# A transformer block on one core: x and the per-layer input also handed over with channels on partitions, and one conversion moved at two boundaries

## The chip, the core and the metric

The kernel runs on one core of a Trainium2 chip. The metric is the device time in microseconds of one execution of the whole program, on inputs that lie in the chip's memory. Five engines work side by side, each through its own list of instructions in order: PE (matrix multiply, results into PSUM), DVE (vector), ACT (activations), POOL, and SP, which here only issues transfers. ACT can issue transfers too.

## The reference, cut to what matters

One decoder layer on 256 tokens with 2048 channels, in float32. The part at the front is

    u    = rmsnorm(x, g_mix_pre)          # per token; gain per channel
    proj = u @ w_in[i]                    # 2048 x 10240
    qa, ka, va, qb, kb, vb, ga, gb = split(proj)

Then come two kinds of attention, two branch products that are mixed by sigmoid gates, `w_out`, a residual and a norm, an MLP (`w_up`, squared relu, `w_down`), a residual and a norm, and last `sigmoid(rmsnorm(h) @ w_ple_gate) * (p @ w_ple_proj)` with a norm and a residual, where `p` is the per-layer input, 256 tokens by 256 channels.

## The kernel before

PE contracts over partitions, so an activation has to stand with its channels on partitions. The kernel computes every product with its factors in two parts: a float32 is split into a high part (rounded to the type PE takes at full rate) and a low part (the rest), and three products hi·hi, hi·lo, lo·hi are summed in PSUM.

Weights come in slices of 256 rows by 512 columns (512 KB), `raw`, into a pool of five buffers (`NRAW`). `head` makes the high part `whi` on ACT, `low` the low part `wlo` on DVE; these have eight buffers. A *chunk* is one product of 512 output columns; with 2048 channels it has eight *steps* s = 0..7, each of one raw slice, and each step has two halves m = 0, 1 (128 tokens each). A half is six matmuls, so a step is twelve. `run` walks the steps; ahead of each half it calls the chunk's `hook(s, m)`, then `ensure`, which issues loads and conversions in order up to a slice ahead of the step, then the matmuls, then the functions of the chunk's `script`. Nothing reorders: the order in which Python calls the engines is the order on each engine, and semaphores do the rest. Transfers take eight semaphores in turn, so each transfer also waits until the eighth before it has landed.

The first chunk, `c_in[0]`, is special. x is loaded token by token on partitions (`load_x`, 512 channels at a time), turned by PE with an identity (`turn`, four 128x128 transposes into PSUM), and `turned` then scales it by the gain of each channel while it splits it into `uT.hi` (ACT, line 188) and `uT.lo` (DVE, line 190). Three pairs of such transposes stand between steps of `c_in[0]` (its `script`). The squares of x for the norm are taken from the same tile (line 604), and the resulting factor `rs1` is applied only when a product leaves PSUM. The gains themselves come as rows of 128 and are turned by PE too (`setup_gain`). The small constants are loaded by `load_small`.

The per-layer input p is turned the same way much later (`turn_p`, inside the first chunk of `w_out`), and is used by the chunks `pp_ch`.

A `Boundary` stands where a norm ends one stage and starts the next, once before `w_up` and once before `w_ple_gate`. While two short chunks `pps[0]`, `pps[1]` and the first half-steps of the next chunk keep PE going, the residual is added (`A`, DVE line 754), the result turned (`T`, PE) and split (`U`, ACT and DVE line 190), and the next chunk's first weights are converted (`H` on ACT, `L` on DVE line 234). The `script` tables set the order. The next chunk runs its steps 0 to 5 with m = 0 first (`lead=6`), so it needs weights up to step 5 before it needs the second half of the tokens.

Of the kernel before, what the change touches and what calls it, by code (L numbers as in the profile page):

```python
# [23 lines left out]
DFF = 8192  # L24
PLE = 256
# [5 lines left out]
CW = 512  # L31
# [14 lines left out]
C_END = 512  # L46
# [33 lines left out]
def tile_hybrid_block(ctx: ExitStack, tc: tile.TileContext, a, out: bass.AP):  # L80
    nc = tc.nc
    pe, act, dve = nc.tensor, nc.scalar, nc.vector

    x_d = a["x"][0]
    p_d = a["p"][0, 0]
# [10 lines left out]
    def aux(name):  # L96
        return ps.tile([P, 512], F32, name=name, tag="aux", bufs=4)
# [5 lines left out]
    gT = [cst.tile([P, NT], F32, name=f"gT{i}") for i in range(3)]  # L103
    gr = [cst.tile([NT, P], F32, name=f"gr{i}") for i in range(3)]
# [3 lines left out]
    nc.sync.dma_start(con[:, 0:P], a["consts"][:, 0:P])  # L108
    nc.scalar.dma_start(gr[0], a["g_mix_pre"][0].rearrange("(k p) -> k p", p=P))

    def load_small():
        for i, g in ((1, "g_mlp_pre"), (2, "g_ple_pre")):
            nc.sync.dma_start(gr[i], a[g][0].rearrange("(k p) -> k p", p=P))
        nc.sync.dma_start(con[:, P:C_END], a["consts"][:, P:C_END])
# [4 lines left out]
    def setup_gain(i):  # L119
        g_ps = aux("g_ps")  # L120
        pe.transpose(g_ps[:, 0:NT], gr[i], ident[0:NT, 0:NT])
        dve.tensor_copy(gT[i], g_ps[:, 0:NT])
# [463 lines left out]
    def load_x(kg):
        nc.sync.dma_start(x_sb[kg // 2][:, kg % 2], x_d[:, kg * CW:(kg + 1) * CW].rearrange("(m p) c -> p m c", p=P))

    xt = {}

    def turn_x(kg):
        xt.update({mm: turn(x_sb[kg // 2][:, kg % 2, mm]) for mm in range(2)})

    def first(s, m):
        kg = (s + 1) // 2
        if s % 2 == 0:
            if m and kg < 2:
                load_x(kg + 2)
        elif kg < 4 and m == 0:
            for mm in range(2):  # L600
                turned(xt[mm], uT, kg, mm, 0)
        for k, mm in {3: ((0, m),), 5: ((1, m),), 6: ((2, m),), 7: ((3, 0), (3, 1)) if m == 0 else ()}.get(s, ()):
            junk = at.tile([P, CW], F32, name="junk", tag="t1", bufs=1)
            act.activation(junk, x_sb[k // 2][:, k % 2, mm], AF.Square, accum_out=ss1[:, mm, k:k + 1])
        if (s, m) == (5, 1):
            load_small()
        if (s, m) == (7, 0):
            ss1t = sm.tile([P, 2], F32, name="ss1t", bufs=1)
            dve.tensor_reduce(ss1t, ss1, AX.X, ALU.add)
            rstd(ss1t, D, rs1, "x")  # L610

    z = sm.tile([P, P], F32, name="z", tag="w2", bufs=4)
    dve.memset(z, 0.0)

    def warm(n, more=False):
        if not more:
            state["warm"] = aux("warm")
        w = state["warm"]
        for i in range(n):
            pe.matmul(w[:, 0:P], lhsT=z, rhs=z, start=True, stop=True)  # L620

    for j in range(2):
        nc.sync.dma_start(x_sb[0][:, 0, 0, j * 256:(j + 1) * 256], x_d[0:P, j * 256:(j + 1) * 256])
        load(0, j)
    nc.scalar.dma_start(x_sb[0][:, 0, 1], x_d[P:T, 0:CW])
    loads(2)
    load_x(1)
    warm(4)
    setup_gain(0)
    warm(3)  # L630
    t0 = aux("t_ps")
    xt[0] = t0.rearrange("p (j t) -> p j t", j=4)
    for j in range(2):
        for i in range(2 * j, 2 * j + 2):
            pe.transpose(t0[:, i * P:(i + 1) * P], x_sb[0][:, 0, 0, i * P:(i + 1) * P], ident)
        warm(1, j)
        head(0, j)
        low(0, j)
        turned(xt[0], uT, 0, 0, 0, range(2 * j, 2 * j + 2))
    xt[1] = turn(x_sb[0][:, 0, 1])  # L640
    turned(xt[1], uT, 0, 1, 0)
    state["head"] = state["conv"] = 1
    c_in[0].hook = first
    c_in[0].script = {(2 * g, 1): [lambda g=g: turn_x(g + 1)] for g in range(3)}
    c_in[0].ahead = lambda s, m: (2 * m, 2, 2, 2, 2, 2, 4, 5)[s]

    for c in order1:
        if c is g_ch[2, 0]:
            while tasks:
                tick()  # L650
            ph2.close()
            at2 = ph1.enter_context(tc.tile_pool(name="at2", bufs=1))
            for n in range(2):
                for wh in range(2):
                    act.activation(G[n][:, wh], G[n][:, wh], AF.Sigmoid)
        if c is br[0, 0]:
            mT = Tbuf("A", "m")
        c.post = c.make()
        run(c)
        if c is c_in[0]:  # L660
            setup_lambda()
            setup_gain(1)
            setup_gain(2)


    def settle(s, m):

        nonlocal b2, h, og, pTh, pTl
        if (s, m) != (4, 0):
            return  # L670
        while tasks:
            tick()
        ph1.close()
        b2 = ctx.enter_context(tc.tile_pool(name="b2", bufs=1))
        h = [b2.tile([P, D], F32, name=f"h{m}") for m in range(2)]
        og = [b2.tile([P, D], F32, name=f"og{m}", tag=f"og{m}", bufs=1) for m in range(2)]
        p_sb = sm.tile([P, 2, PLE], F32, name="p_sb", tag="w2", bufs=4)
        nc.sync.dma_start(p_sb, p_d.rearrange("(m p) c -> p m c", p=P))
        pTh = b2.tile([P, 2, T], F32R, name="pTh")
        pTl = b2.tile([P, 2, T], F32R, name="pTl")  # L680
        start(turn_p(p_sb))
        o_ch[0].post = post_out(0)

    def turn_p(p_sb):
        for _ in range(7):
            yield
        for i in range(2):
            nc.sync.dma_start(h[i], x_d[i * P:(i + 1) * P, :])
        p_ps = aux("pl_ps")
        for m in range(2):  # L690
            for j in range(2):
                pe.transpose(p_ps[:, (j * 2 + m) * P:(j * 2 + m + 1) * P], p_sb[:, m, j * P:(j + 1) * P], ident)
# [306 lines left out]
```

## Time and profile before

| | |
|---|---|
| runs of the kernel | 1494.03, 1493.86, 1492.85 us, median 1493.86 |
| the profiled execution | 1494.14 us |
| its span, first to last instruction | 1492.3 us |
| around the span | 1.84 us |
| PE busy | 1476.8 us, 99% of the span |
| DVE and ACT busy | 860.6 us (58%) and 710.4 us (48%) |
| transfers | 282.14 MB, mean 189 GB/s |

PE is busy almost throughout, and the chain of work that ended last runs over PE for 96% of the span. What is not PE in it lies at the start, at the two boundaries and at the end. A busy PE counts a matmul from its start to its modelled end, and neighbours overlap, so the time between two starts is the better measure of what one costs.

### The profile page before, as it was taken

The page shows a single profiled execution, that of the slowest core. Times are in us where ns is not written, and L with a number is a line of the kernel's source. Part 1 is how long each engine was busy: PE and PEld are TensorE (multiplying, and loading weights), DVE is VectorE, ACT ScalarE, POOL GpSimd, SP SyncE. Part 2 cuts the span into 40 slices and gives each one's busy share as a digit, 9 for nine tenths or more (in the row PEclk, how much of TensorE's full clock was granted, in tenths as well). Part 3 has the DMA queues.
Part 4 walks back from the last instruction along what each step waited for, and adds up shares of the span by engine and source line. Part 5 has one row for each costly group of instructions (what it writes and reads, how often), then busy time and mean ns, then how long its engine had stood idle before and what let it go on. Part 6 is the DMA issues. An engine that isn't in the chain of part 4 may idle for free.

```text
span 1492.3 us, 18552 instructions
## 1 busy us (share of the span) xinstructions
PE 1476.8 (99%) x7117; PEld 1239.1 (83%) x7117; DVE 860.6 (58%) x1111; ACT 710.4 (48%) x995; POOL 0.2 (0%) x4
## 2 busy tenths in 40 slices
PE   9999999999999999999999999999999999999997
PEld 7888888888888888888888888888888888888786
DVE  5664646565444665557664456545655546655865
ACT  6654445454544443447544445433444334544752
POOL 0000000000000000000000000000000000000000
PEclk9999999999999999999999999999999999999999
DMA  8755555555566556745566555666456656466471
GB/s 264 262 160 182 165 178 164 180 162 186 156 217 209 176 189 220 255 147 184 183 227 194 185 184 184 200 195 198 156 197 210 195 159 213 158 228 223 132 230 57
DMA packets 146537, 282.14 MB, mean 189 GB/s; under 512 B 8928, under 2 KB 10896, under 8 KB 146192
## 3 DMA queue, kind: packets, MB, share of 16 engines
q1 hardware_dynamic: 145984, 280.28, 58.2%
q8 instruction: 56, 0.92, 0.3%
q10 hardware_dynamic: 464, 0.66, 0.2%
q14 instruction: 33, 0.27, 0.1%
HBM read 278.81 MB, written 2.10 MB: 188 GB/s over the span
## 4 chain that ended last, share of the span: by engine, by line
PE 96%; DVE 2%; ACT 1%; DMA 0%; issue 0%; SPq 0%; DVEq 0%; ACTq 0%
PE acc L296 23%; PE acc L297 23%; PE acc L295 23%; PE acct L323 15%; PE acct L324 8%; PE t_ps L177 1%; PE s_ps L398 1%; DVE h L754 1%; PE acc L960 1%; PE acc L961 1%; PE acc L959 1%; PE qk_ps L366 0%; DVE u L190 0%; DVE wlo L234 0%; DMA raw<-in_w_in 0%; ACT u L188 0%
## 5 line engine op out<-in xcount | busy, mean ns | idle before, releaser
L234 DVE TENSOR_TENSOR wlo<-raw,whi 128x1024 fp32r<-128x1024 f32 (+1 forms) x518 | 617.7, 1218 | 428.2 <-ACT whi L228 427.7
L228 ACT ACTIVATE whi<-raw 128x1024 fp32r<-128x1024 f32 (+1 forms) x518 | 532.6, 1053 | 410.9 <-PE acc L297 285.4
L323 PE MATMUL acct<-u,whi 128*128 128x512 f32 x960 | 338.3, 398 | 0.0
L295 PE MATMUL acc<-whi,u 128*128 128x512 f32 x768 | 306.6, 399 | 0.0
L296 PE MATMUL acc<-wlo,u 128*128 128x512 f32 x768 | 300.2, 391 | 1.9 <-DVE wlo L234 1.8
L297 PE MATMUL acc<-whi,u 128*128 128x512 f32 x768 | 300.4, 391 | 0.0
L324 PE MATMUL acct<-u,wlo 128*128 128x256 f32 x960 | 269.0, 280 | 0.0
L323 PEld LDWEIGHTS acct<-u,whi 128*128 128x128 f32 x960 | 180.3, 188 | 44.4
L295 PE MATMUL acc<-whi,h 128*128 128x512 f32 x512 | 199.3, 389 | 0.0
L296 PE MATMUL acc<-wlo,h 128*128 128x512 f32 x512 | 199.3, 389 | 0.0
L297 PE MATMUL acc<-whi,h 128*128 128x512 f32 x512 | 199.3, 389 | 0.0
L324 PEld LDWEIGHTS acct<-u,wlo 128*128 128x128 f32 x960 | 181.2, 189 | 0.2
L296 PEld LDWEIGHTS acc<-wlo,u 128*128 128x128 f32 x768 | 144.9, 189 | 31.7 <-DVE wlo L234 2.9
L297 PEld LDWEIGHTS acc<-whi,u 128*128 128x128 f32 x768 | 144.6, 188 | 30.6
L295 PEld LDWEIGHTS acc<-whi,u 128*128 128x128 f32 x768 | 144.9, 189 | 28.5
L295 PEld LDWEIGHTS acc<-whi,h 128*128 128x128 f32 x512 | 96.1, 188 | 20.0
L297 PEld LDWEIGHTS acc<-whi,h 128*128 128x128 f32 x512 | 96.1, 188 | 20.0
L296 PEld LDWEIGHTS acc<-wlo,h 128*128 128x128 f32 x512 | 96.1, 188 | 19.8
L852 ACT ACTIVATE r<-acct 128x256 f32<-128x256 f32 x60 | 22.8, 380 | 68.0 <-PE acct L324 68.0
L853 DVE TENSOR_TENSOR r<-acct,r 128x256 f32<-128x256 f32 x60 | 24.5, 422 | 47.5 <-ACT r L852 47.5
L295 PE MATMUL acc<-whi,o 128*128 128x512 f32 x128 | 50.4, 394 | 0.0
L295 PE MATMUL acc<-whi,m 128*128 128x512 f32 x128 | 50.1, 392 | 0.0
(163 smaller groups left out, 991.0 us busy)
## 6 DMA issues: line engine op xcount, KB each, us to landing
raw<-in_w_in SPq DMA_DIRECT2D x159, 512.0 KB, 4.3
raw<-in_w_up SPq DMA_DIRECT2D x128, 512.0 KB, 4.2
raw<-in_w_down SPq DMA_DIRECT2D x128, 512.0 KB, 5.5
raw<-in_w_out SPq DMA_DIRECT2D x32, 512.0 KB, 5.7
raw<-in_w_ple_gate SPq DMA_DIRECT2D x32, 512.0 KB, 5.7
raw<-in_w_br_moba SPq DMA_DIRECT2D x16, 512.0 KB, 4.3
raw<-in_w_br_diff SPq DMA_DIRECT2D x16, 512.0 KB, 4.7
h<-in_x SPq DMA_DIRECT2D x2, 1024.0 KB, 10.3
```

Source lines behind the costliest of these rows:

```text
L177: pe.transpose(t_ps[:, j * P:(j + 1) * P], src[:, j * P:(j + 1) * P], ident)
L228: act.activation(hi[:, j], raw[:, j], AF.Copy)
L234: dve.tensor_sub(lo[:, j], raw[:, j], hi[:, j].bitcast(F32))
L295: pe.matmul(acc[m], lhsT=ah, rhs=hi[:, j, :], start=first, stop=False)
L296: pe.matmul(acc[m], lhsT=ah, rhs=lo[:, j, :], start=False, stop=False)
L297: pe.matmul(acc[m], lhsT=al, rhs=hi[:, j, :], start=False, stop=last)
L323: pe.matmul(acc[q].rearrange("p a t -> p (a t)"), lhsT=hi[:, j, ws], rhs=mv, start=first, stop=False)
L324: pe.matmul(acc[q][:, 0], lhsT=lo[:, j, ws], rhs=mv[:, 0:T], start=False, stop=last)
L398: pe.matmul(s_ps[:, j, :], lhsT=q[:, h, m * P:(m + 1) * P], rhs=k[:, h, 0:w], start=True, stop=True)
L754: dve.scalar_tensor_tensor(h[m][:, s], og[m][:, s], self.r[m], h[m][:, s], op0=ALU.mult, op1=ALU.add)
L852: act.activation(r[:, q % 2], acc[:, 1], AF.Copy)
L853: dve.tensor_add(r[:, q % 2], acc[:, 0], r[:, q % 2])
```

## The change

x is handed over a second time as `xT`, channels on partitions, each partition's data in one piece; p is handed over only in that layout (`pT`), and the three gains as one small table `gT` with channels on partitions. The layouts are made on the host, without arithmetic.

The first chunk then reads `xT`: `scaled` takes two 128x256 tiles (all tokens of two groups of channels) from SBUF, and makes `uT.hi` and `uT.lo` with one ACT and one DVE instruction per tile. The transposes of x, of p and of the gains are gone. The squares still need tokens on partitions, so x is loaded a second time by rows: `load_xs` brings 512 channels as two tiles of 128x512 (one per token half) in a pool tag `w2` that has four buffers, and `square_x` squares them in place. At both boundaries `L(5)` moves ahead of `A(1, 2)`, `A(1, 3)` and `U(0, 3)`.

```
-    def load_x(kg): ...          # x by rows, 512 KB
-    def turn_x(kg): ...          # PE transposes
+    def load_xT(a0, b0, eng=nc.sync):
+        eng.dma_start(x_sb[a0 // 8][:, a0 % 8:a0 % 8 + b0 - a0], a["xT"][:, a0:b0])
+
+    def scaled(*kts):
+        for kt in kts:
+            act.activation(uT.hi[kt // 4][:, kt % 4], x_sb[kt // 8][:, kt % 8], AF.Copy, scale=gT[0][:, kt:kt + 1])
+        for kt in kts:
+            dve.scalar_tensor_tensor(uT.lo[kt // 4][:, kt % 4], x_sb[kt // 8][:, kt % 8], gT[0][:, kt:kt + 1],
+                                     uT.hi[kt // 4][:, kt % 4].bitcast(F32), op0=ALU.mult, op1=ALU.subtract)
+
+    def load_xs(kg):
+        for m in range(2):
+            xs[kg, m] = sm.tile([P, CW], F32, name="xs", tag="w2", bufs=4)
+            nc.sync.dma_start(xs[kg, m], x_d[m * P:(m + 1) * P, kg * CW:(kg + 1) * CW])
+
+    def square_x(kg):
+        for m in range(2):
+            t = xs.pop((kg, m))
+            act.activation(t, t, AF.Square, accum_out=ss1[:, m, kg:kg + 1])
+
     def first(s, m):
...
+        if m == 0:
+            if s + 2 < 8:
+                scaled(2 * s + 4, 2 * s + 5)
+            if s == 7:
+                square_x(3)
...
+            return
+        if s == 0:
+            load_xT(8, 12)
+            load_xT(12, 16)
+        if 3 <= s < 6:
+            square_x(s - 3)
+        if 1 <= s < 5:
+            load_xs(s - 1)
+        if s == 5:
+            load_small()
...
+    load_xT(0, 2, nc.scalar)
...
     for j in range(2):
         load(0, j)
+    load_xT(2, 4)
+    loads(1)
+    load_xT(4, 8)
     loads(2)
+    for i in range(10):
+        pe.matmul(w[:, 0:P], lhsT=z, rhs=z, start=True, stop=True)
+    scaled(0, 1)
     for j in range(2):
         head(0, j)
         low(0, j)
+    scaled(2, 3)
...
-        p_sb = sm.tile([P, 2, PLE], F32, name="p_sb", tag="w2", bufs=4)
-        nc.sync.dma_start(p_sb, p_d.rearrange("(m p) c -> p m c", p=P))
+        p_sb = sm.tile([P, 2, T], F32, name="p_sb", tag="w2", bufs=4)
+        nc.sync.dma_start(p_sb, a["pT"])
...
-                pe.transpose(p_ps[:, (j * 2 + m) * P:(j * 2 + m + 1) * P], p_sb[:, m, j * P:(j + 1) * P], ident)
-        yield
-        split(pTh, pTl, p_ps.rearrange("p (j t) -> p j t", j=2))
+        split(pTh, pTl, p_sb)
...
-                             (0, 1): [T(0, 3), H(5), L(4), A(1, 2), A(1, 3), U(0, 3), L(5)]}
+                             (0, 1): [T(0, 3), H(5), L(4), L(5), A(1, 2), A(1, 3), U(0, 3)]}
```

SP's list in the first chunk of the kernel before, from the load of raw slice 3 on. The x rows are the last loads of x, the raw rows are slices 3 to 7 of `w_in`; a row waits for a landing (DMAHW) and where a buffer is used again for the engine that read it (DVE, the low part).

```order
L210 DMA raw_214<-in_w_in 128x2x512 [waits DMAHW3_49]
L210 DMA raw_232<-in_w_in 128x2x512 [waits DMAHW4_49]
L587 DMA x1_99<-in_x 128x2x512 [waits DMAHW5_49]
L210 DMA raw_279<-in_w_in 128x2x512 [waits DMAHW6_49,DVE_49]
L210 DMA raw_299<-in_w_in 128x2x512 [waits DMAHW7_49,DVE_49]
L210 DMA raw_345<-in_w_in 128x2x512 [waits DMAHW0_49,DVE_49]
```

The same place of the changed kernel; raw_170 is slice 3 and raw_278 slice 7, and the xs rows are the row-wise loads of x, two for each 512 channels.

```order
L201 DMA raw_170<-in_w_in 128x2x512 [waits DMAHW2_49]
L593 DMA xs_182<-in_x 128x512 [waits DMAHW3_49]
L593 DMA xs_184<-in_x 128x512 [waits DMAHW4_49]
L201 DMA raw_196<-in_w_in 128x2x512 [waits DMAHW5_49]
L593 DMA xs_208<-in_x 128x512 [waits DMAHW6_49]
L593 DMA xs_210<-in_x 128x512 [waits DMAHW7_49]
L201 DMA raw_222<-in_w_in 128x2x512 [waits DMAHW0_49,DVE_49]
L593 DMA xs_236<-in_x 128x512 [waits DMAHW1_49,Activation_49]
L593 DMA xs_238<-in_x 128x512 [waits DMAHW2_49,Activation_49]
L201 DMA raw_250<-in_w_in 128x2x512 [waits DMAHW3_49,DVE_49]
L593 DMA xs_264<-in_x 128x512 [waits DMAHW4_49,Activation_49]
L593 DMA xs_266<-in_x 128x512 [waits DMAHW5_49,Activation_49]
```

Four xs tiles go out between the slices without an engine to wait for; the fifth and later ones (xs_236 on) wait for ACT, and slices 6 and 7 stand behind them. ACT's list of the changed kernel around the first squares, where whi_224 is the high part of slice 5 and whi_252 that of slice 6:

```order
L219 ACTIVATE whi_224<-raw_222 128x1024 [waits DMAHW0_49]
L598 ACTIVATE xs_182,ss1_95<-xs_182 128x512 [waits DMAHW3_49]
L598 ACTIVATE xs_184,ss1_95<-xs_184 128x512 [waits DMAHW4_49]
L583 ACTIVATE u3_87<-x1_93,gT_73 128x256 [waits DMAHW1_49]
L583 ACTIVATE u3_87<-x1_93,gT_73 128x256
L219 ACTIVATE whi_252<-raw_250 128x1024 [waits DMAHW3_49]
L598 ACTIVATE xs_208,ss1_95<-xs_208 128x512 [waits DMAHW6_49]
L598 ACTIVATE xs_210,ss1_95<-xs_210 128x512 [waits DMAHW7_49]
```

The squares of the first 512 channels stand behind the conversion of slice 5, those of the next behind that of slice 6. DVE's list at the second boundary, before (wlo the low parts of steps 4, 5 and 6 of the next chunk, h the additions, u the splits):

```order
L234 TENSOR_TENSOR wlo<-raw,whi 128x1024
L754 SCALAR_TENSOR_TENSOR h_4598<-og_4600,r_10934,h_4598 128x512 x2
L190 SCALAR_TENSOR_TENSOR u_10279<-t_ps,gT_75,u_10279 128x128 x4
L234 TENSOR_TENSOR wlo<-raw,whi 128x1024
L190 SCALAR_TENSOR_TENSOR u_10276<-t_ps,gT_75,u_10276 128x128 x4
```

and with the change:

```order
L225 TENSOR_TENSOR wlo<-raw,whi 128x1024 x2
L742 SCALAR_TENSOR_TENSOR h_4517<-og_4519,r_10848,h_4517 128x512 x2
L181 SCALAR_TENSOR_TENSOR u_10193<-t_ps,gT,u_10193 128x128 x4
L181 SCALAR_TENSOR_TENSOR u_10190<-t_ps,gT,u_10190 128x128 x4
L181 SCALAR_TENSOR_TENSOR u_10191<-t_ps,gT,u_10191 128x128 x4
```

The low part of step 5 now stands right behind that of step 4, and two additions and four splits come one low part later; the rows behind them stand where they stood.

## Rows read from the trace of the kernel before

**Rows 1.** The page: the span, and busy time of an engine

```profile
span 1492.3 us, 18552 instructions
PE 1476.8 (99%) x7117; PEld 1239.1 (83%) x7117; DVE 860.6 (58%) x1111; ACT 710.4 (48%) x995; POOL 0.2 (0%) x4
```

**Rows 2.** Timeline of PE in the first chunk: start us, us, instruction

```profile
9.77 0.78 PE L295 MATMUL acc<-whi,u 128*128 128x512 f32 x1
...
13.76 0.42 PE L295 MATMUL acc<-whi,u 128*128 128x512 f32 x1
...
14.25 0.39 PE L297 MATMUL acc<-whi,u 128*128 128x512 f32 x1
...
15.28 0.47 PE L295 MATMUL acc<-whi,u 128*128 128x512 f32 x1
...
30.13 0.39 PE L295 MATMUL acc<-whi,u 128*128 128x512 f32 x1
...
36.02 0.39 PE L297 MATMUL acc<-whi,u 128*128 128x512 f32 x1
...
36.56 0.50 PE L295 MATMUL acc<-whi,u 128*128 128x512 f32 x1
36.90 0.40 PE L296 MATMUL acc<-wlo,u 128*128 128x512 f32 x1
```

**Rows 3.** Timeline of SP: issue of raw slices 5 to 7

```profile
9.08 6.11 SPq L210 DMA_DIRECT2D raw<-in_w_in  x3
```

**Rows 4.** Transfers issued from 9.0 to 9.2 us: KB, us to landing

```profile
raw<-in_w_in SPq DMA_DIRECT2D x1, 512.0 KB, 9.4
```

**Rows 5.** Transfers, 8 to 18 us

```profile
DMA packets 2045, 3.94 MB, mean 394 GB/s; under 512 B 122, under 2 KB 122, under 8 KB 2045
```

**Rows 6.** Raw slices, 45 to 150 us: ns min/median/max, and issue to landing

```profile
L228 ACT ACTIVATE whi<-raw x40: 1040/1052/1065, 44.7 to 148.1; 128x1024 fp32r<-128x1024 f32 x40
L234 DVE TENSOR_TENSOR wlo<-raw,whi x40: 1215/1225/1227, 45.8 to 149.2; 128x1024 fp32r<-128x1024 f32 x40
L210 SPq DMA_DIRECT2D raw<-in_w_in x39: 367/368/476, 47.0 to 147.7; - x39
...
DMA to landing us min/median/max: 3.5/4.3/5.4
```

**Rows 7.** Timeline of ACT: squares of x

```profile
35.67 0.61 ACT L604 ACTIVATE junk<-x 128x512 f32<-128x512 f32 x1
...
36.41 0.63 ACT L604 ACTIVATE junk<-x 128x512 f32<-128x512 f32 x1
```

**Rows 8.** Windows, 1482 to 1492 us: PE, PEld, DVE, ACT, POOL, PEclk, DMA share, GB/s

```profile
1482.00:1492.00 10.00, 0.09 (x1) 0.00 (x0) 5.38 (x15) 0.98 (x3) 0.00 (x0) 0.65 0.46 160
```

**Rows 9.** Timeline of PE around the transposes of p

```profile
597.68 0.39 PE L297 MATMUL acc<-whi,m 128*128 128x512 f32 x1
...
598.27 0.48 PE L295 MATMUL acc<-whi,m 128*128 128x512 f32 x1
598.58 0.40 PE L296 MATMUL acc<-wlo,m 128*128 128x512 f32 x1
```

**Rows 10.** Timeline of PE at step 5 behind the two boundaries

```profile
679.15 0.48 PE L295 MATMUL acc<-whi,u 128*128 128x512 f32 x1
680.06 0.50 PE L296 MATMUL acc<-wlo,u 128*128 128x512 f32 x1 [0.43 <-DVE wlo L234]
...
1398.41 0.60 PE L177 MATMUL t_ps<-con,h 128*128 128x128 f32 x4
1398.77 0.48 PE L295 MATMUL acc<-whi,u 128*128 128x512 f32 x1
1400.64 0.50 PE L296 MATMUL acc<-wlo,u 128*128 128x512 f32 x1 [1.39 <-DVE wlo L234]
```

**Rows 11.** Timeline of DVE at the second boundary

```profile
1397.02 1.40 DVE L754 SCALAR_TENSOR_TENSOR h<-og,r,h 128x512 f32<-128x512 f32 x2
...
1399.38 1.21 DVE L234 TENSOR_TENSOR wlo<-raw,whi 128x1024 fp32r<-128x1024 f32 x1
```

More of the change, by code (lines that the diff above doesn't have):

```diff
@@ L102, in tile_hybrid_block @@
     mask = con[:, C_MASK:C_MASK + 2 * P]
-    gT = [cst.tile([P, NT], F32, name=f"gT{i}") for i in range(3)]
-    gr = [cst.tile([NT, P], F32, name=f"gr{i}") for i in range(3)]
+    gall = cst.tile([P, 3, NT], F32, name="gT")
+    gT = [gall[:, i] for i in range(3)]
     lamv = cst.tile([P, 4, HD], F32, name="lamv")
@@ L107, in tile_hybrid_block @@
     lam = cst.tile([P, 1], F32, name="lam")
-    nc.sync.dma_start(con[:, 0:P], a["consts"][:, 0:P])
-    nc.scalar.dma_start(gr[0], a["g_mix_pre"][0].rearrange("(k p) -> k p", p=P))
+    nc.scalar.dma_start(gall, a["gT"])
     def load_small():
-        for i, g in ((1, "g_mlp_pre"), (2, "g_ple_pre")):
-            nc.sync.dma_start(gr[i], a[g][0].rearrange("(k p) -> k p", p=P))
-        nc.sync.dma_start(con[:, P:C_END], a["consts"][:, P:C_END])
+        nc.sync.dma_start(con, a["consts"])
         for i, n in enumerate(("lambda_q1", "lambda_k1", "lambda_q2", "lambda_k2")):
@@ L117, in load_small @@
         nc.sync.dma_start(gsub, a["diff_subln_g"][0:1, :].to_broadcast([P, 2 * HD]))
[L119 to L122, printed above, removed]
     def setup_lambda():
@@ L340, in tile_hybrid_block @@
     oT = Tbuf("B", "o")
-    x_sb = [gp.tile([P, 2, 2, CW], F32, name=f"x{i}", tag="xg", bufs=2) for i in range(2)]
+    x_sb = [gp.tile([P, 8, T], F32, name=f"x{i}", tag="xg", bufs=2) for i in range(2)]
     rs1 = cst.tile([P, 2], F32, name="rs1")
@@ L584, in tile_hybrid_block @@
     ss1 = sm.tile([P, 2, 4], F32, name="ss1", bufs=1)
[L586 to L592, printed above, removed]
-    def first(s, m):
[L595 to L605, printed above, removed]
-            load_small()
[L607 to L610, printed above, removed]
@@ L612, in tile_hybrid_block @@
-    z = sm.tile([P, P], F32, name="z", tag="w2", bufs=4)
-    dve.memset(z, 0.0)
[L615 to L620, printed above, removed]
+    def load_xT(a0, b0, eng=nc.sync):
[6 more added lines that the diff above has]
+                                     uT.hi[kt // 4][:, kt % 4].bitcast(F32), op0=ALU.mult, op1=ALU.subtract)
@@ new lines, in tile_hybrid_block @@
+    xs = {}
+    def load_xs(kg):
[6 more added lines that the diff above has]
+            act.activation(t, t, AF.Square, accum_out=ss1[:, m, kg:kg + 1])
+    def first(s, m):
+        if m == 0:
[3 more added lines that the diff above has]
+                square_x(3)
+                ss1t = sm.tile([P, 2], F32, name="ss1t", bufs=1)
+                dve.tensor_reduce(ss1t, ss1, AX.X, ALU.add)
+                rstd(ss1t, D, rs1, "x")
+            return
[7 more added lines that the diff above has]
+        if s == 5:
+            load_small()
@@ L622, in tile_hybrid_block @@
+    load_xT(0, 2, nc.scalar)
+    z = sm.tile([P, P], F32, name="z", bufs=1)
+    dve.memset(z, 0.0)
+    act.activation(sm.tile([P, 1], F32, name="z1", bufs=1), z[:, 0:1], AF.Copy)
+    w = aux("warm")
     for j in range(2):
-        nc.sync.dma_start(x_sb[0][:, 0, 0, j * 256:(j + 1) * 256], x_d[0:P, j * 256:(j + 1) * 256])
         load(0, j)
-    nc.scalar.dma_start(x_sb[0][:, 0, 1], x_d[P:T, 0:CW])
+    load_xT(2, 4)
+    loads(1)
+    load_xT(4, 8)
     loads(2)
-    load_x(1)
-    warm(4)
@@ L629, in tile_hybrid_block @@
[L629 to L632, printed above, removed]
+    for i in range(10):
+        pe.matmul(w[:, 0:P], lhsT=z, rhs=z, start=True, stop=True)
+    scaled(0, 1)
     for j in range(2):
-        for i in range(2 * j, 2 * j + 2):
-            pe.transpose(t0[:, i * P:(i + 1) * P], x_sb[0][:, 0, 0, i * P:(i + 1) * P], ident)
-        warm(1, j)
         head(0, j)
         low(0, j)
-        turned(xt[0], uT, 0, 0, 0, range(2 * j, 2 * j + 2))
-    xt[1] = turn(x_sb[0][:, 0, 1])
@@ L641, in tile_hybrid_block @@
-    turned(xt[1], uT, 0, 1, 0)
+    scaled(2, 3)
     state["head"] = state["conv"] = 1
     c_in[0].hook = first
-    c_in[0].script = {(2 * g, 1): [lambda g=g: turn_x(g + 1)] for g in range(3)}
     c_in[0].ahead = lambda s, m: (2 * m, 2, 2, 2, 2, 2, 4, 5)[s]
@@ L661, in tile_hybrid_block @@
             setup_lambda()
-            setup_gain(1)
-            setup_gain(2)
     def settle(s, m):
@@ L688, in turn_p @@
             nc.sync.dma_start(h[i], x_d[i * P:(i + 1) * P, :])
-        p_ps = aux("pl_ps")
-        for m in range(2):
-            for j in range(2):
-                pe.transpose(p_ps[:, (j * 2 + m) * P:(j * 2 + m + 1) * P], p_sb[:, m, j * P:(j + 1) * P], ident)
-        yield
-        split(pTh, pTl, p_ps.rearrange("p (j t) -> p j t", j=2))
+        split(pTh, pTl, p_sb)
     b2 = h = og = pTh = pTl = None
@@ L975, in tile_hybrid_block, with by_partition @@
         tick()
-_INS = ["x", "p", "w_in", "w_br_moba", "w_br_diff", "w_out", "lambda_q1", "lambda_k1", "lambda_q2", "lambda_k2",
-        "diff_subln_g", "g_mix_pre", "g_mix_post", "w_up", "w_down", "g_mlp_pre", "g_mlp_post", "w_ple_proj",
-        "w_ple_gate", "g_ple_pre", "g_ple_post"]
+_INS = ["x", "w_in", "w_br_moba", "w_br_diff", "w_out", "lambda_q1", "lambda_k1", "lambda_q2", "lambda_k2",
+        "diff_subln_g", "g_mix_post", "w_up", "w_down", "g_mlp_post", "w_ple_proj", "w_ple_gate", "g_ple_post"]
+def by_partition(v):
+    return np.ascontiguousarray(v.reshape(-1, P, v.shape[-1]).transpose(1, 0, 2))
 def kernel(**inputs):
@@ L990 @@
     given["consts"] = shape_constants()
+    given["xT"] = by_partition(inputs["x"][0].T)
+    given["pT"] = by_partition(inputs["p"][0, 0].T)
+    given["gT"] = np.ascontiguousarray(
+        np.stack([inputs[g][0].reshape(NT, P).T for g in ("g_mix_pre", "g_mlp_pre", "g_ple_pre")], 1))
     for name, v in given.items():
```

1 line of the change is left out of this document (removed).

## The prediction

> **What bounds the kernel now.** I read the page first, then PE's waits and its timeline where it waits, then the transfers of the first 45 us. PE is busy for 99% of the span [rows 1], so only what PE does or waits for can change the time. Matmuls of the first chunk start 5.89 us / 26 = 0.2265 us apart in full flow (30.13 to 36.02, [rows 2]), so a step of twelve takes 2.72 us. The first nine take 0.443 us each (9.77 to 13.76): PE ran at its 1.2 GHz level until about 13.8 us and at 2.4 GHz after it. That slow start costs 9 x 0.217 = 1.95 us. The gap for eight transposes is 15.28 - 14.25 = 1.03 us [rows 2]. The second chunk starts at 36.56. Transfers run at 394 GB/s early on [rows 5], which is 512 KB in 1.33 us, twice as fast as PE uses raw slices up. At the two boundaries PE waits for the low part of step 5 [rows 10].
>
> **The first chunk, removed.** The transposes, the gains' turns and a part of the start leave PE. If nothing took their place, this would be worth several us (third rival). I do not count it, because of what is added.
>
> **The first chunk, added.** x comes twice. Up to raw slice 5, the kernel before issues 5192 KB (SP's and ACT's lists together), the changed one 6168 KB, of which 1024 KB are xs tiles. Slice 5 landed at 9.08 + 9.4 = 18.5 us [rows 3, 4]; 976 KB more at 394 GB/s are 2.5 us [rows 5], so it lands at 21.0.
>
> Now the order decides. The pool `w2` has four buffers, and the xs tiles 0 to 3 fill it. Tile 4 must wait until tile 0 is squared. The squares stand on ACT behind the conversion of slice 5, and SP's list has slice 6 behind xs tiles 4 and 5. Queued behind that wait on SP are slice 6, two more xs tiles, slice 7, the small constants, and slice 8 of the next chunk; behind slice 6 on ACT are its conversion and the next squares, and PE waits for that conversion. Step by step:
>
> - ACT converts slice 5 from 21.0 to 22.05 (1.05 us, [rows 6]), and squares at 0.74 us each (35.67 to 36.41, [rows 7]): first square done 22.8, second 23.55.
> - SP issues xs tile 4 at 22.8, tile 5 at 23.55, each 0.37 us or somewhat more [rows 6], slice 6 at 23.95. By then nothing is in flight. A raw slice takes 3.5 to 5.4 us to land, median 4.3 [rows 6]; I take 4.3, because half a megabyte goes out just ahead. Slice 6 lands at 28.25.
> - ACT converts it by 29.3, DVE has the low part at 30.5 (1.225 us, [rows 6]). PE finished step 5 at about 25.8 (low part of slice 5 at 23.3, then 11 x 0.2265). It idles 3.5 us, does one matmul, idles another 1.0, and ends step 6 at 33.0.
> - The same again: squares done 30.05 and 30.8, slice 7 issued 31.2, landed 35.5, converted 36.55, low part 37.8. PE ends step 7 at 37.8 + 2.5 = 40.3.
> - Slice 8 follows 640 KB of small loads: 1152 KB at 394 GB/s, 3.0 us, 38.5 (up to 39.5 if the small ones are slow). Its low part is there at 40.8, the second matmul would want it at 40.5: 0.3 more. From slice 9 on, transfers gain on PE again.
>
> So the second chunk runs 40.3 + 0.3 - 36.56 = 4.0 us later, less 0.1 for its first matmul, which now follows no transpose (36.56 to 36.90 against 0.2265, [rows 2]): **+3.9 us**. Bounds: 3.5 us for both landings gives 1.6 less, 5.4 gives 2.2 more, slow small loads 1.0 more.
>
> The Trainium skill, page "DMA: Bandwidth & Descriptors", section "Anatomy of one DMA — SWDGE (gpsimd) path", fits a transfer as about 2.0 us plus bytes over 436 GB/s, for the POOL path. By that the 1 MB that goes out from 22.8 on would land at 27.2 and not 28.25, and the sum below would be 2.1 us lower, 1494.9. The trace does not bear it out: a lone 512 KB would be 3.2 us, and the shortest row is 3.5.
>
> **The clock.** After the last matmul, which ends at 1482.09, the granted clock averages 0.65 over 10 us [rows 8]: with the two levels, 7.0 us at 1.2 GHz, so it fell 2.9 us after PE stopped. Both holes here begin with a longer idle time (3.5 us each). A fall in the first costs little, since step 6 at 1.2 GHz takes 5 us of a time in which PE would idle anyway. A fall in the second, or one not yet undone, slows the matmuls from 37.8 on. Bounds: nothing, and 1.95 us (the slow stretch at the start). I take **+1.3 us**, nearer to the upper one because both holes are longer than 2.9 us.
>
> **p.** Four transposes go, in the middle of a chunk of `w_out`: 598.27 - 597.68 = 0.59 and 0.31 for the next start, against 2 x 0.2265 [rows 9]: **-0.45 us**. The split of p reads SBUF instead of PSUM, off PE's path.
>
> **The boundaries.** Step 5's second matmul comes 0.91 us after the first (679.15 to 680.06), and at the second boundary 1.87 us (1398.77 to 1400.64), where 0.31 us is usual behind transposes [rows 9, 10]. The low part now runs 1.2 us or more earlier and is there in time. First boundary: -0.6. At the second, the additions start at 1397.02 + 1.13 = 1398.15 (1.13 us is the low part's step from one start to the next) and the first is done at 1398.85 (1.40 us for two, [rows 11]); the transposes that PE began at 1398.41 need it and start at 1398.9: 1.56 - 0.5, so -1.05. The split U(0, 3) comes 1.13 us later, but its matmuls come after six half-steps of the other tokens; everything behind it on DVE stands as before. **-1.65 us**, bounds -2.2 (no new wait) and 0 (both waits replaced).
>
> **Costed at nothing.** ACT and DVE make the 16 tiles of u from SBUF in single instructions of twice the width; they lie in ACT's waits for raw slices. Ten warming matmuls and the tiny extra ACT instruction lie ahead of the first landing. The late `rs1` delays only the emptying of the first chunk's sums; PSUM has four such buffers, and the third chunk needs them some 20 us later. Without this cover each is below 1 us.
>
> **Sum.** 3.9 + 1.3 - 0.45 - 1.65 = +3.1 us on the profiled execution's 1494.14 (span 1492.3 and 1.84 around it) is 1497.2. The median of the runs is 0.28 below the profiled one: **1497.0 us**, 0.2% slower. A difference under 0.2% (3.0 us) cannot be told from none here, so the forecast lies on that bound.
>
> **Rivals.**
> - *The holes are there, but the clock holds, or recovers inside them, and slices land after 3.5 to 4.3 us.* For it: the second hole gets shorter if step 6 is slow. Then the sum is 0.2 to 1.8: 1494.1 to 1495.7, no change. Chance 0.28.
> - *Landings near 5.4 us, the small loads slow, the clock slow:* 3.9 + 2.2 + 1.0 and the other terms, about 1500.2. For it: several transfers share the queue. Chance 0.10.
> - *No hole, faster:* if slice 6 could pass the waiting xs tiles, or the squares came early, slices would follow at the queue's rate: 6 at 23.7, 7 at 26.4, 8 at 29.4, its low part at 31.7 where PE used it at 36.90: -5.2, with the rest -7.3, **1486.6 us**. It decides if slice 6 is issued before about 20 us. Against it: slices 5 to 7 took 6.11 us to issue in the kernel before [rows 3], each waiting, none passing. The Trainium skill says the same ("DMA: Bandwidth & Descriptors", "Anatomy of one DMA — SWDGE (gpsimd) path"): a semaphore wait is served by the issuing sequencer, before dispatch. The lists show the order. Chance 0.05.
> - *The forecast,* the holes with a clock that falls: 1496.0 to 1499.0, chance 0.57.
>
> **Chances and range.** Slower by over 0.2% (above 1496.85): four fifths of the forecast, all of the second rival: 0.55. Within 0.2%: the first rival and the rest: 0.39. Faster: 0.06. The range from 1494.5 to 1499.8 leaves out the third rival and the ends of the first two. The likeliest case's own range is 1496.0 to 1499.0.
>
> **What would show it.** In the trace of the changed kernel: SP idle from about 14 to 22.8 us with xs tile 4 released by ACT; ACT idle some 4 us before the conversions of slices 6 and 7; two holes of 3 to 4 us on PE at steps 6 and 7; the second chunk starting near 40.5; no wait at step 5 behind the first boundary and one of half a microsecond at the transposes behind the second; 0.63 us matmuls behind the second hole if the clock fell. It is wrong if slice 6 is issued early, if the holes are under 2 us, or if the second chunk starts before 36.5.

## The result and the profile after

The changed kernel takes 1504.51 us (median of 6 runs, 1504.06 to 1505.36) against 1493.23 us of the kernel before (6 runs): 1.0076 of it, 95% interval 1.0063 to 1.0089. It is slower, as forecast, but by 11.3 us instead of 3.1; 1497.0 was forecast and the range ended at 1499.8. The two profiled executions lie 10.15 us apart (1504.29 and 1494.14).

The page of the changed kernel, its span and the busy time of an engine:

```profile
span 1502.5 us, 18457 instructions
PE 1478.6 (98%) x7080; PEld 1238.6 (82%) x7080; DVE 858.9 (57%) x1092; ACT 708.9 (47%) x980; POOL 0.2 (0%) x4
```

PE's busy time grew by 1.8 us with 37 instructions fewer [rows 1], the span by 10.2: most of the loss is idle time of PE. Its waits in the changed kernel (what it waited for, us in total, times, longest):

```profile
PE acc L286 <- ACT whi L219: 10.1, 4, 3.6
PE acc L287 <- DVE wlo L225: 1.9, 4, 0.8
PE t_ps L168 <- DVE h L742: 0.6, 2, 0.4
```

One of the four waits for whi, 1.97 us, stands ahead of the first matmul; the other three are the holes below. PE's timeline in the changed kernel from the end of step 5 on (start, duration, instruction, in brackets the idle time ahead and who ended it), and behind it the place of p and the two boundaries:

```profile
25.16 0.39 PE L288 MATMUL acc<-whi,u 128*128 128x512 f32 x1
29.15 0.79 PE L286 MATMUL acc<-whi,u 128*128 128x512 f32 x1 [3.60 <-ACT whi L219]
30.41 0.79 PE L287 MATMUL acc<-wlo,u 128*128 128x512 f32 x1 [0.47 <-DVE wlo L225]
...
37.64 0.51 PE L286 MATMUL acc<-whi,u 128*128 128x512 f32 x1 [2.41 <-ACT whi L219]
38.90 0.80 PE L287 MATMUL acc<-wlo,u 128*128 128x512 f32 x1 [0.76 <-DVE wlo L225]
...
46.08 0.79 PE L286 MATMUL acc<-whi,u 128*128 128x512 f32 x1 [2.12 <-ACT whi L219]
47.34 0.79 PE L287 MATMUL acc<-wlo,u 128*128 128x512 f32 x1 [0.47 <-DVE wlo L225]
...
52.05 0.39 PE L286 MATMUL acc<-whi,u 128*128 128x512 f32 x1
...
610.23 0.39 PE L288 MATMUL acc<-whi,m 128*128 128x512 f32 x1
610.45 0.39 PE L286 MATMUL acc<-whi,m 128*128 128x512 f32 x1
...
691.16 0.48 PE L286 MATMUL acc<-whi,u 128*128 128x512 f32 x1
691.48 0.39 PE L287 MATMUL acc<-wlo,u 128*128 128x512 f32 x1
...
1410.29 0.66 PE L168 MATMUL t_ps<-con,h 128*128 128x128 f32 x4 [0.35 <-DVE h L742]
1410.70 0.48 PE L286 MATMUL acc<-whi,u 128*128 128x512 f32 x1
1411.02 0.39 PE L287 MATMUL acc<-wlo,u 128*128 128x512 f32 x1
```

Set beside the same instructions of before, the rows tell where the time went. The matmul ahead of p starts 12.55 us later (610.23 against 597.68, [rows 9]): that is what the start, the first chunk and the first step of the second cost. The next one is 12.18 us later (598.27), so p gave 0.37 there. Ahead of step 5 behind the first boundary the lag is 12.01 (691.16 against 679.15, [rows 10]; the 0.17 since p is spread over many matmuls), and it falls to 11.42, a gain of 0.59; by the second matmul of step 5 behind the second boundary it is 10.38 (1411.02 against 1400.64), 1.04 less. Everything outside the first 52 us came as forecast; the first 52 us cost 12.55 and not 5.2.

There are three holes and not two, and the third stands at the second chunk. The chain of work that ended last in that stretch (start, us, what) shows each step:

```profile
20.02 1.06 ACT whi L219
21.08 1.23 ACT xs L598 x4
...
22.33 0.33 SPq L593
...
22.75 5.26 DMA raw<-in_w_in
...
28.04 1.06 ACT whi L219
29.09 1.24 ACT xs L598 x4
...
30.35 4.87 DMA xs<-in_x
...
35.27 9.59 DMA raw<-in_w_in
...
44.97 1.06 ACT whi L219
```

Up to 30 us it reads as forecast: conversion of slice 5, squares, xs tile, slice 6. Then comes a piece that was forecast to be over by 38.5, or 39.5 with slow small loads: raw slice 8, 9.59 us from issue to landing. Slice 7 was issued at 30.77 and took 5.7 us (landed 36.5), slice 8 landed 8.4 us behind it, at 44.87. Between them on the queue lie the small loads. The transfers of the changed kernel that SP issued from 31.6 to 34.0 us (KB each, median us from issue to landing):

```profile
lamv<-in_lambda_q SPq DMA_DIRECT2D x2, 64.0 KB, 5.7
lamv<-in_lambda_k SPq DMA_DIRECT2D x2, 64.0 KB, 6.9
gsub<-in_diff_subln_g SPq DMA_DIRECT2D x1, 128.0 KB, 9.7
```

gsub is issued at 33.89 and so lands at 43.55, and slice 8 1.3 us behind it.

### The profile page after: what moved, and what is told of

It reads as the page before. It is cut to its first block, busy times and chain, and to the rows that moved or that the text cites. A ratio compares the mean times of both kernels' runs of the same rounds, so it can differ in the third digit from the quotient of the medians.

```text
span 1502.5 us, 18457 instructions
## 1 busy us (share of the span) xinstructions
PE 1478.6 (98%) x7080; PEld 1238.6 (82%) x7080; DVE 858.9 (57%) x1092; ACT 708.9 (47%) x980; POOL 0.2 (0%) x4
## 3 DMA queue, kind: packets, MB, share of 16 engines
q1 hardware_dynamic: 146272, 282.36, 57.9%
## 4 chain that ended last, share of the span: by engine, by line
PE 95%; DMA 2%; DVE 1%; ACT 1%; SPq 0%; issue 0%; DVEq 0%; ACTq 0%
PE acc L288 23%; PE acc L287 23%; PE acc L286 23%; PE acct L314 15%; PE acct L315 8%; DMA raw<-in_w_in 2%; PE t_ps L168 1%; PE s_ps L389 1%; DMA x<-in_xT 1%; PE acc L948 0%; PE acc L949 0%; PE acc L947 0%; PE qk_ps L357 0%; DMA xs<-in_x 0%; DVE h L742 0%; ACT whi L219 0%
## 5 line engine op out<-in xcount | busy, mean ns | idle before, releaser
L287 PE MATMUL acc<-wlo,u 128*128 128x512 f32 x768 | 303.3, 395 | 2.0 <-DVE wlo L225 1.9
L286 PEld LDWEIGHTS acc<-whi,u 128*128 128x128 f32 x768 | 146.1, 190 | 40.8 <-ACT whi L219 11.9
```

Source lines behind the costliest of these rows:

```text
L286: pe.matmul(acc[m], lhsT=ah, rhs=hi[:, j, :], start=first, stop=False)
L287: pe.matmul(acc[m], lhsT=ah, rhs=lo[:, j, :], start=False, stop=False)
```

## The experiments

Theory one: two things make the loss, the wait of xs tile 4 with slices 6 and 7 behind it, and the small loads, which hold slice 8 up. Against it stand: the second reading of x (2 MB more) is what makes everything late; a transfer issued so late takes 9 us in any case; and, for the rest, the clock.

**The wait of xs tile 4.** Eight buffers instead of four:

```diff
-            xs[kg, m] = sm.tile([P, CW], F32, name="xs", tag="w2", bufs=4)
+            xs[kg, m] = sm.tile([P, CW], F32, name="xs", tag="w2", bufs=8)
```

(and the same number wherever that tag stands, also for tiles used much later).

> The changed kernel with eight buffers instead of four in the pool that the xs tiles use; the order of every engine stays. Theory one (the wait of xs tile 4 for ACT's square, with slices 6 and 7 behind it on SP): the waits of PE for whi at steps 6 and 7 (3.6 and 2.4 us) go, slice 6 is issued before 18 us instead of 22.75. The small loads behind slice 7 still take 6 to 8 us in the queue, so slice 8 lands at 32 to 35 us and the second chunk's second matmul starts at 35 to 37 us (47.34 in the changed kernel, 36.90 before): 10 to 12 us less, 1491 to 1494 us. Theory two (the second reading of x, 2 MB more, holds the slices up, whoever waits): slice 6 lands no earlier than 26 us, the holes stay within 1 us of their size, 1501 us or more.

Measured: 1492.3 us, 0.9992 of the kernel before (0.9983 to 1.0001), 12.2 us less than the changed kernel. PE's timeline at the second chunk, and the transfer of slice 8, which is issued at 24.20:

```profile
30.82 0.39 PE L288 MATMUL acc<-whi,u 128*128 128x512 f32 x1
34.57 0.50 PE L286 MATMUL acc<-whi,u 128*128 128x512 f32 x1 [3.36 <-ACT whi L219]
35.83 0.71 PE L287 MATMUL acc<-wlo,u 128*128 128x512 f32 x1 [0.76 <-DVE wlo L225]
```

```profile
raw<-in_w_in SPq DMA_DIRECT2D x1, 512.0 KB, 9.2
```

The holes at steps 6 and 7 are gone and PE runs through the first chunk to 30.82, although x is still read twice: the bytes are not the cause of these two holes. Slice 6 was issued at 15.38. What stays is the wait for slice 8.

**The same wait, on another queue.** The four buffers stay; POOL issues the xs tiles:

```diff
-            nc.sync.dma_start(xs[kg, m], x_d[m * P:(m + 1) * P, kg * CW:(kg + 1) * CW])
+            nc.gpsimd.dma_start(xs[kg, m], x_d[m * P:(m + 1) * P, kg * CW:(kg + 1) * CW])
```

> The changed kernel with the xs tiles issued by POOL instead of SP; four buffers as in the changed kernel, so xs tile 4 waits for ACT's square as before, but on a queue of its own. If what costs is that slices 6 and 7 stand behind that wait: slice 6 is issued before 18 us, the holes at steps 6 and 7 go, only the hole at slice 8 behind the small loads stays, as with eight buffers: 1491 to 1495 us. If it is the wait itself or the bytes: the holes stay, 1501 us or more.

Measured: 1492.03 us, 0.9996 (0.9987 to 1.0005). The timelines of POOL and of SP in this run:

```profile
23.22 1.15 POOL L593 DMA_DIRECT2D xs<-in_x  x2 [19.70 <-ACT xs L598]
```

```profile
7.37 9.66 SPq L201 DMA_DIRECT2D raw<-in_w_in  x5
```

xs tile 4 still waits, 19.70 us, for ACT's square; but the five raw slices on SP, 3 to 7, are all issued by 17.1 us. The wait as such costs nothing; what stands behind it on its queue does. One more thing differs here: on POOL the first four xs tiles go out from 1.25 us on, ahead of slices 3 to 7. And since the pool has four buffers throughout, the gain with eight does not come from the other tiles of that tag. (The Trainium skill, page "DMA: Bandwidth & Descriptors", section "Anatomy of one DMA — SWDGE (gpsimd) path", says that a semaphore wait is served by the issuing sequencer before dispatch; the trace agrees on both queues: ACT's square of tile 0 ends at 21.70 in the changed kernel and SP issues tile 4 at 21.72, here at 22.93 and POOL issues it at 23.22.)

**The small loads, moved away.** con stays; the five others are issued at step 3 of the second chunk, and the small computation on DVE and ACT that reads them comes two chunks later:

```diff
         nc.sync.dma_start(con, a["consts"])
+
+    def load_rows(s, m):
+        if (s, m) != (3, 1):
+            return
         for i, n in enumerate(("lambda_q1", "lambda_k1", "lambda_q2", "lambda_k2")):
...
     c_in[0].hook = first
+    c_in[1].hook = load_rows
...
-        if c is c_in[0]:
+        if c is c_in[2]:
             setup_lambda()
```

> The changed kernel with the five broadcast loads (lamv four times, gsub) moved from step 5 of the first chunk to step 3 of the second; con stays. Theory one (these 384 KB hold slice 8 up in the queue): the holes at steps 6 and 7 stay, slice 8 lands 2 to 3 us behind slice 7 (near 39 us instead of 44.87), PE's third wait for whi (2.1 us) and the low part's behind it go, and the clock has come back by the second chunk: 3 to 5.5 us less, 1499 to 1501.5 us. Theory two (slice 8 is late because any transfer issued then takes over 9 us to land): slice 8 still lands 8 us behind slice 7, and the time stays at 1504 us.

Measured: 1500.25 us, 1.0046 (1.0031 to 1.0061). Slice 8, issued at 33.07, landed after 6.9 us, 2.0 us behind slice 7; PE waited for whi three times instead of four. The late transfer itself is not slow.

**What is slow in them.** First two wide transfers from arrays that hold each row 128 times:

```diff
-        for i, n in enumerate(("lambda_q1", "lambda_k1", "lambda_q2", "lambda_k2")):
-            nc.sync.dma_start(lamv[:, i, :], a[n][0:1, :].to_broadcast([P, HD]))
-        nc.sync.dma_start(gsub, a["diff_subln_g"][0:1, :].to_broadcast([P, 2 * HD]))
+        nc.sync.dma_start(lamv, a["lam_rows"])
+        nc.sync.dma_start(gsub, a["g_rows"])
```

> The changed kernel with lamv and gsub read from arrays in which the row already stands 128 times, in two transfers with 2 KB and 1 KB per partition, instead of five that read one row 128 times; the bytes and their place on the queue stay. If the five are slow because they are many, in small packets or read one row over and over: 384 KB take about 1 us, slice 8 lands near 40 us, as with the rows moved away, 1499 to 1502 us. If it is the bytes alone or the place in the queue: slice 8 lands at 43 us or later, 1503 to 1504.5 us.

Measured: 1499.39 us, 1.0039 (1.0024 to 1.0054); slice 8 landed 3.1 us behind slice 7. That leaves the number of transfers, their small packets and the repeated address. So the five transfers as they were, each from an array of its own that holds the row 128 times:

```diff
-            nc.sync.dma_start(lamv[:, i, :], a[n][0:1, :].to_broadcast([P, HD]))
-        nc.sync.dma_start(gsub, a["diff_subln_g"][0:1, :].to_broadcast([P, 2 * HD]))
+            nc.sync.dma_start(lamv[:, i, :], a["rows_" + n])
+        nc.sync.dma_start(gsub, a["rows_diff_subln_g"])
```

> The changed kernel with lamv and gsub still in five transfers of 512 B and 1 KB per partition, at the same place of the queue, but each from an array in which the row stands 128 times, so that no address is read twice. If reading one row over and over is what was slow: slice 8 lands 3 to 4 us behind slice 7, as in the run with the two wide transfers (3.1), PE's third hole goes, 1499 to 1500.5 us. If it is the small packets or the number of transfers: slice 8 lands 7 us or more behind slice 7 (8.4 in the changed kernel), 1502.5 us or more.

Measured: 1499.16 us, 1.0042 (1.0026 to 1.0057). The small transfers in this run, and slice 8, issued at 34.78:

```profile
lamv<-in_rows_lambda_q SPq DMA_DIRECT2D x2, 64.0 KB, 5.9
lamv<-in_rows_lambda_k SPq DMA_DIRECT2D x2, 64.0 KB, 5.7
gsub<-in_rows_diff_subln_g SPq DMA_DIRECT2D x1, 128.0 KB, 5.1
...
raw<-in_w_in SPq DMA_DIRECT2D x1, 512.0 KB, 5.3
```

Number, size, place and bytes are those of the changed kernel, and so is the number of packets on the queue over the whole execution (146272); gsub lands after 5.1 us instead of 9.7, and slice 8 3.1 us behind slice 7 instead of 8.4. What differs is the source, one row read 128 times. But not every such load is dear. The landings (issue plus time to landing, us):

| | slice 7 | con | lambda_q1 | lambda_k1 | lambda_q2 | lambda_k2 | gsub | slice 8 |
|---|---|---|---|---|---|---|---|---|
| changed kernel | 36.50 | 37.19 | 37.39 | 38.47 | 38.67 | 40.89 | 43.55 | 44.87 |
| this run | 36.91 | 37.60 | 37.87 | 38.13 | 38.36 | 38.58 | 38.80 | 40.06 |

In the changed kernel both loads of lambda_q land 0.2 us behind the load ahead of them, as from rows of their own; both of lambda_k and gsub take 6.0 of the 6.4 us. The runs with eight buffers, with POOL and with idle matmuls (below) show the same two cheap loads. What sets the dear ones apart, no run shows.

**The same in the kernel before.** There the small loads lie between slices 7 and 8 too. The edit is that of the last run.

> The kernel before with one edit: lamv and gsub from arrays in which the row stands 128 times. If the repeated row costs the queue as much there and is only hidden: slice 8, which landed 6.4 us behind slice 7 (21.19 to 27.58), lands 3 to 4 us behind it, PE does not wait for it in either, and the time stays within 0.1% of the kernel before. If the queue is slow only in the changed kernel, where SP issues late: slice 8 lands as before, 6 us or more behind slice 7.

Measured: 1493.0 us, 1.0001 (0.9991 to 1.0010). Slice 8 of the kernel before and of this run, both issued near 21.7 (21.63 and 21.76):

```profile
raw<-in_w_in SPq DMA_DIRECT2D x1, 512.0 KB, 6.0
```

```profile
raw<-in_w_in SPq DMA_DIRECT2D x1, 512.0 KB, 4.1
```

The landings again:

| | slice 7 | con | lambda_q1 | lambda_k1 | lambda_q2 | lambda_k2 | gsub | slice 8 |
|---|---|---|---|---|---|---|---|---|
| kernel before | 21.19 | 21.93 | 22.20 | 22.41 | 22.62 | 22.91 | 26.22 | 27.58 |
| this run | 21.31 | 21.94 | 22.17 | 22.43 | 22.78 | 24.23 | 24.61 | 25.89 |

With slice 7 landing at 21.19 and 21.31, slice 8 came 6.4 and 4.6 us behind it. (In the run with the boundaries alone, below, which starts like the kernel before, it came 6.0 us behind.) That lies between what the two cases of the expectation ask for, 3 to 4 and 6 or more: SP issues gsub only at 21.33 there, and I take it that the late issues make the rest. So a price was there in the kernel before, some 1.3 to 1.8 us and not the 5.3 of the changed kernel; it stands at gsub, while the four lambda loads landed 0.2 to 0.3 us apart in the kernel before. PE, whose second chunk starts at 36.56 [rows 2], never saw it.

**The clock.** Matmuls on data of no use ahead of steps 6 and 7 and of the second chunk:

```diff
+    def fill(n):
+        f = aux("fill")
+        for _ in range(n):
+            pe.matmul(f[:, 0:P], lhsT=z, rhs=z, start=True, stop=True)
...
+        if (s, m) in ((6, 0), (7, 0)):
+            fill({6: 34, 7: 44}[s])
...
+    c_in[1].hook = lambda s, m: fill(44) if (s, m) == (0, 0) else None
```

> The changed kernel with 34, 44 and 44 small matmuls on data of no use ahead of steps 6 and 7 and of the second chunk, so that PE works through most of the three holes; the landings stay. If PE's idle time brings the clock down: the matmuls behind the holes start 0.23 us apart instead of 0.43, but what is won at steps 6 and 7 goes into the next wait, since the landings set it; only the second chunk's first step is shorter, 2.0 to 2.4 us less, 1502 to 1502.5 us. If the clock falls whatever PE does: the spacing behind the holes stays at 0.43, and the time stays at 1504.5 us or is up to 2 us more.

Measured: 1513.39 us, 1.0137 (1.0121 to 1.0154): 9 us more. I had mis-sized them; 34 of them take 7.5 us, twice the hole. PE's waits for whi fall to 2.3 us in total, so this run does not price the clock; it shows that matmuls which outlast the hole cost more than they bring. With 15, 19 and 19:

> The changed kernel with 15, 19 and 19 idle matmuls (0.22 us each at full clock, by the run with 34, 44 and 44, which outlasted the holes) ahead of steps 6 and 7 and of the second chunk; the landings stay. If idle time brings the clock down: the matmuls of these steps start 0.2265 us apart, the second chunk's second matmul still at 47 to 48 us since slice 8's landing sets it, its first step 2.0 to 2.4 us shorter: 1501.5 to 1502.8 us. If not: 1504.5 us.

Measured: 1502.38 us, 1.0061 (1.0047 to 1.0075), 2.1 us less than the changed kernel. The windows from 46 to 52 us (busy time of PE, PEld, DVE, ACT, POOL, then the granted clock, DMA share and GB/s), the changed kernel first:

```profile
46.00:52.00 6.00, 5.45 (x12) 3.98 (x13) 5.34 (x14) 5.27 (x9) 0.00 (x0) 0.51 0.84 282
```

```profile
46.00:52.00 6.00, 5.24 (x27) 4.21 (x26) 4.95 (x11) 5.42 (x9) 0.00 (x0) 1.00 0.87 302
```

The granted clock is 0.51 (near the 1.2 GHz level) in the changed kernel and 1.00 (2.4 GHz) here. The second and the thirteenth matmul of the second chunk in this run:

```profile
47.84 0.50 PE L287 MATMUL acc<-wlo,u 128*128 128x512 f32 x1 [0.77 <-DVE wlo L225]
...
50.49 0.39 PE L286 MATMUL acc<-whi,u 128*128 128x512 f32 x1
```

The intervals of the two ratios overlap, so the size is better read here: 2.65 us between the two starts, against 4.71 in the changed kernel (47.34 to 52.05). So the clock is worth 2.1 us in the changed kernel, and its idle time brought it down.

**The boundaries alone.** The kernel before with the low part of step 5 moved:

```diff
-                             (0, 1): [T(0, 3), H(5), L(4), A(1, 2), A(1, 3), U(0, 3), L(5)]}
+                             (0, 1): [T(0, 3), H(5), L(4), L(5), A(1, 2), A(1, 3), U(0, 3)]}
```

> The kernel before with one edit: the low part of step 5 ahead of the additions at both boundaries. By my terms 0.6 us less at the first and 1.05 at the second, 1.65 in all, 1491.3 us. If another wait takes the place of each: within 0.3 us of before.

Measured: 1491.14 us, 0.9988 (0.9979 to 0.9996), 2.4 us less in the medians with 1.65 inside the interval. PE at the two places:

```profile
678.06 0.48 PE L295 MATMUL acc<-whi,u 128*128 128x512 f32 x1
678.37 0.39 PE L296 MATMUL acc<-wlo,u 128*128 128x512 f32 x1
...
1397.19 0.66 PE L177 MATMUL t_ps<-con,h 128*128 128x128 f32 x4 [0.35 <-DVE h L754]
1397.61 0.48 PE L295 MATMUL acc<-whi,u 128*128 128x512 f32 x1
1397.92 0.40 PE L296 MATMUL acc<-wlo,u 128*128 128x512 f32 x1
```

The second matmul follows the first after 0.31 us at both, where it took 0.91 and 1.87 [rows 10]; at the second boundary the transposes wait 0.35 us for an addition.

**Both causes away.** Eight buffers and the two wide transfers:

> Eight buffers for the xs tiles and lamv and gsub from arrays that hold the row 128 times, together. If the two causes found so far are all that holds PE up: slice 8 lands at 28 to 29 us, its low part is there at 30.5 to 31.5, PE comes to it at 30.8 after the first chunk without a hole, the second chunk's second matmul starts at 31 to 32 us (36.90 in the kernel before) and its clock holds; with the 2.1 us of p and the boundaries 7 to 8 us less than before, 1485 to 1486.5 us. If a third thing stands behind them (slices 9 to 12, or the bytes of the second x): a hole of 2 us or more stays in the second chunk, 1488 us or more.

Measured: 1486.38 us, 0.9956 (0.9942 to 0.9970): faster than both kernels, by 7.1 and 18.1 us. PE at the start of its second chunk:

```profile
30.91 0.39 PE L287 MATMUL acc<-whi,u 128*128 128x512 f32 x1
31.14 0.39 PE L285 MATMUL acc<-whi,u 128*128 128x512 f32 x1
31.70 0.50 PE L286 MATMUL acc<-wlo,u 128*128 128x512 f32 x1 [0.17 <-DVE wlo L224]
```

No hole but 0.17 us; slice 8 landed at 29.22. No third cause of that size stands behind the two.

**The slow start.** On top of that, 20 warming matmuls instead of 10:

```diff
-    for i in range(10):
+    for i in range(20):
```

> The kernel with eight buffers and the two wide transfers, and 20 warming matmuls instead of 10 ahead of the first chunk. If idle time ahead of the first matmul (1.4 us there) is why its first eight to ten matmuls run 0.43 us apart: they now start 0.2265 us apart, PE comes to slices 3 to 5 earlier and waits there for their low parts, since the landings stay; what is left at the second chunk is 0 to 1.2 us: 1485.2 to 1486.5 us. If the slow start has another cause: no change, 1486.4 us, or up to 1 us more where the extra matmuls outlast the first landing.

Measured: 1486.46 us, 0.9955 (0.9943 to 0.9968), no change. The first step now runs 0.23 us apart, so what PE does ahead of it makes the slow start; whether it is the idle 1.4 us or the number of warming matmuls, this run does not part, since it changes both. But the first matmul starts 0.5 us later (7.58 against 7.07), and the second chunk begins at 31.57 against 31.14. PE comes to the second step earlier and waits there, 0.75 and 0.23 us, and slices land a little later (slice 7 at 26.1 against 25.6). What the clock gives there, the landings take.

## Why the prediction failed, step by step

The mechanism of the two holes was right, and one term of the sum was far too small. The step that failed is: "Slice 8 follows 640 KB of small loads: 1152 KB at 394 GB/s, 3.0 us, 38.5 (up to 39.5 if the small ones are slow)". From the landing of slice 7 it took 8.4 us instead of the 3.0, and a third hole came of it. The rate of raw slices was applied to transfers that read one row 128 times. With rows of their own the step takes 3.1 us, and the changed kernel 1499.16 us, which lies inside the range. The trace of the kernel before had a sign of it, slice 8 6.4 us behind slice 7 and gsub 3.3 us behind the load ahead of it; the argument passed over it, since PE does not wait for it there. It was no more than a sign: 1.3 to 1.8 us of it are the repeated rows'.

- **The first chunk, +3.9.** The chain is as forecast, link by link: xs tile 4 released by ACT, slice 6 behind it, hole, the same again, with a second hole of 2.4 and not 3 to 4 us, since step 6 ran at the slow clock and ended at 35.2 instead of 33.0. Slice 6 landed at 28.02 (forecast 28.25), but that is luck, through errors that cancel: slice 5 landed 1.0 us earlier than I had it (20.00), the squares took 0.6 us each and not 0.74, and slice 6 took 5.26 us, not 4.3. Slice 7 took 5.7, so the low part of step 7 came at 38.90 instead of 37.8. Then slice 8: the second matmul of the second chunk was due at 40.8 and started at 47.34, 6.5 us late, 1.0 of them from slice 7's landing (36.5, forecast 35.5) and 5.4 from the small loads. The fit of the Trainium skill ("DMA: Bandwidth & Descriptors", "Anatomy of one DMA — SWDGE (gpsimd) path") for the POOL path, about 2.0 us plus bytes over 436 GB/s, gives an estimate of 4.4 us for the 1 MB issued from 21.72 on, taken as one transfer; this trace has 6.3.
- **The clock, +1.3** (bounds 0 and 1.95). From 47.34 the second chunk's matmuls take 4.71 us from the second start to the thirteenth (52.05) instead of 11 x 0.2265 = 2.49: 2.2 lost, and the run with the filled holes gives 2.1 back. That is a little above the upper bound, and at another place than forecast: I had put the 1.3 on step 7, behind the second hole. At steps 6 and 7 the slow clock cost nothing, as I had argued for the first hole: the next landing came later anyway. The loss stands behind the third hole, which the forecast did not have, so that the size came near the bound is partly luck.
- **Together** 6.5 and 0.9 more than forecast make 7.4; with the 5.2 forecast that is 12.6, the 12.55 read above.
- **p, -0.45:** 0.37 between the two matmuls. **The boundaries, -0.6 and -1.05:** 0.59 and 1.04, with 0.35 us of new wait at the transposes of the second, as forecast.
- **The rivals.** "No hole" had the right condition, slice 6 issued before 20 us, and the wrong price: with eight buffers that holds, and the time is 1492.3 and not 1486.6, since slice 8 lands at 33.4 and not 29.4. With rows of their own as well (the two wide transfers) slice 8 lands at 29.22, and the time is 1486.38. The rival with slow landings had the right direction and allowed 1.0 us for the small loads; the others were wrong.

## What to carry to other kernels

A transfer that waits for a buffer holds up all that stands behind it on its queue: list what that is before giving a new kind of tile too few buffers, or put it on a queue where nothing follows. Price small transfers by their own rows and not by the rate of large ones, above all where an earlier version hid them: the cushion that hid them may be what the change takes away. And in this row of holes only what the last one left behind in the clock counted, since behind the others the next landing came later anyway.

## What the runs showed of the hardware

- Reading one row 128 times: the five transfers of 384 KB landed within 6.4 us behind con (37.19 to 43.55); from rows of their own, with the same sizes and count, within 1.2 us (37.60 to 38.80). The 16 DMA engines were not at their limit meanwhile. The windows from 36 to 41 us, the changed kernel first, then the run with rows of their own (the last two numbers are the engines' mean busy share and GB/s):

```profile
36.00:41.00 5.00, 2.61 (x6) 1.92 (x7) 1.23 (x1) 2.28 (x5) 0.00 (x0) 0.72 0.30 71
```

```profile
36.00:41.00 5.00, 2.19 (x5) 1.60 (x6) 1.23 (x1) 3.12 (x6) 0.00 (x0) 0.81 0.97 331
```

While the repeated rows were read, the engines stood idle for most of the time, and the slices behind did not fill it. Why, and why two of the five loads were cheap all the same, stays open.

- In the chain above slice 8 is issued at 35.27, when xs tile 7 has landed (30.35 + 4.87), though slice 8 uses nothing of that tile. It is the program's own wait: its transfers take eight semaphores in turn, and tile 7 is the eighth transfer ahead of slice 8. With eight buffers it is the same: tile 7 landed at 24.14, and slice 8 is issued at 24.20. With two wide transfers in place of the five, the eighth ahead is xs tile 5, landed at 27.82, and slice 8 is issued at 33.80, right behind gsub. No run changed the number of semaphores.
